# A streaming-encoder trunk: the low parts of the mixing weights formed by an accumulating DMA

## The chip, the cores and the metric

The kernel runs on one core of a Trainium2 chip. The metric is the device time of one execution in microseconds (us): before the change the median of three runs is 1188.21 us (1187.47 to 1188.51). The core has a matrix engine (PE, TensorE), three engines for elementwise work (DVE or VectorE, ACT or ScalarE, POOL or GpSimd), and queues that issue DMA transfers: SP's, and here after the change POOL's as well.

## The reference: what is computed

Two layers on 512 tokens of width 1024, in float32. Each layer has a mixing half and a feed-forward half:

```
h    = rms_norm(x, g_pre_mix)
proj = h @ w_in            # pool 512 | q 512 | k 512 | v 512 | indexer 584
a    = causal pooling mixer (windows 2, 4, 8, 16) @ w_pool * pool_scale
b    = attention of 8 heads over the 128 best keys per query, picked by the indexer
x    = x + rms_norm(concat(a, b) @ w_out, g_post_mix)
h    = rms_norm(x, g_pre_ffn)
x    = x + rms_norm(relu(h @ w_ff1)**2 @ w_ff2, g_post_ffn)
```

## The kernel before

**High and low parts.** PE's operands are F32R tiles, rounded from float32. Each operand is held as two of them: high = the value rounded to F32R, and low = value - high. A product is three matmuls (`mm3`, L825): high x high, high x low, low x high. So each weight has to be loaded, rounded and subtracted before PE may use both parts.

**The weight stream** (`WeightStream`, L420). All weights of both layers pass in a fixed order through one stream: index, q, k, v, pool, output projection (once for each of two pairs of token tiles), then feed-forward. A load brings two chunks of 128 rows (512 KB, or twice 256 KB for the pool weights) into one of NRAW = 2 raw buffers, `wraw`. A chunk is split by `_split` (L519) into one of NWS = 8 weight tiles `ws`, which hold the high part in `[:, 0]` and the low part in `[:, 1]`:

```
self.copy(w[:, 0, :n], raw)                                             # L533
self.tt(w[:, 1, :n], raw, w[:, 0, :n].bitcast(F32), OP.subtract)        # L534
```

`copy` (L656) may go to DVE or to ACT; `tt` (L648) is always DVE. A raw buffer is free again after both subtractions, and `_ahead` then issues the next load on SP's queue. A weight tile is free when its matmuls are done: `ws.done()` splits the next chunk.

**The stages of a layer.** The index projection and the indexer's scores; then q, k and v (`rows_block`, L948: 12 matmuls of 512 columns per chunk), while DVE picks the best keys (`select`, L931, with max and match-replace on tiles `m` and `bias`); `attention(2)`, the pooling mixer, `attention(3)`, `attention(0)`, `attention(1)`; then the output projection `out_pair(1)` and `out_pair(0)` (L1082: 6 matmuls per chunk, since each chunk serves two token tiles), with norms behind each token tile. A norm takes a power on POOL (tile `rstd`, L780). The feed-forward half has other chunks: a part of its weights are sums of blocks (`_combine`, L539, from `uraw`).

**What sets the order.** Every instruction is first recorded with its cost and dependencies (`_Recorder`, L359), then a list scheduler (`Planner`, L83) plans all engines by these costs and latencies in 40 sweeps and issues each engine's instructions in the order of their planned starts (L193). Where there are two ways (`planner.either`, L143), it picks the engine. At run time each engine works through its own list in order and waits where something is not ready.

Profile lines all read L372, the recorder's call; so groups are told apart by tiles: `pg`, `pool`, `pi`, `po`, `s`, `pf`, `one`, `two` are results of matmuls, `pt`, `tr`, `hT` transposes, `early` and `A` left operands.

Of the kernel before, what the change touches and what calls it, by code (L numbers as in the profile page):

```python
# [12 lines left out]
F32 = mybir.dt.float32  # L13
F32R = mybir.dt.float32r
I32 = mybir.dt.int32
AF = mybir.ActivationFunctionType
OP = mybir.AluOpType

P = 128
# [18 lines left out]
POOL_PAIRS = ((2, 3), (0, 1))  # L38
# [44 lines left out]
class Planner:  # L83
# [19 lines left out]
    def __init__(self, nc):  # L103
        self.nc = nc
        self.ops = []
        self.writer, self.readers = {}, {}
        self.rings, self.before, self.first = {}, {}, {}
        self.touched = {}
        self.collected = None
        self.loads = []  # L110
# [75 lines left out]
        self.ops.append((ways, deps, soft - deps))  # L186

    def lag(self, ea, eb):
        if eb == "sp":
            return self.DMA_STARTS  # L190
        return self.DMA_LANDS if ea == "sp" else self.LATENCY.get((ea, eb), 150)

    def issue(self):  # L193
# [13 lines left out]
        for i in range(n - 1, -1, -1):  # L207
            e, cost = ops[i][0][0][:2]
            tail = 0.0
            for j, hard in succ[i]:  # L210
                tail = max(tail, rank[j] + (self.lag(e, ops[j][0][0][0]) if hard else -cost))
            rank[i] = cost + tail
# [146 lines left out]
class _Recorder:  # L359
# [3 lines left out]
    def __getattr__(self, method):  # L363
        def call(*args, **kw):
            out = kw["out"] if "out" in kw else args[0]
            writes = [out] + ([kw["accum_out"]] if kw.get("accum_out") is not None else [])
            if method == "tensor_tensor_reduce":
                writes.append(args[7])
            reads = [a for k, a in list(enumerate(args))[1:] + list(kw.items())
                     if isinstance(a, bass.AP) and k not in ("out", "accum_out") and all(a is not w for w in writes)]  # L370
            way = (self.name, self.cost(method, args, kw, out, reads),
                   lambda: getattr(self.real, method)(*args, **kw), self.port(method, out, reads))  # L372
            if self.planner.collected is not None:
                self.planner.collected.append(way + (writes, reads))
            else:
                self.planner.record([way], writes, reads)
        return call
# [11 lines left out]
    def cost(self, method, args, kw, out, reads):  # L389
        def free(ap):  # L390
            return math.prod(c for _, c in list(ap.ap)[1:])

        def psum(ap):
            return ap.space == bass.MemoryType.PSUM

        n = free(out)
        scalars = sum(free(a) == 1 and n > 1 for a in reads)
        if self.name == "pe":
            if method == "transpose":
                return 59 if args[1].dtype == F32R else 109  # L400
            return max(4.5 + n / 2.25, 111 if free(args[1]) > 64 else 60)
        if self.name == "act":
            accum = kw.get("accum_out") is not None
            return (53 if any(psum(a) for a in reads[:1]) else 93) + n / 1.2 + 93 * (accum + scalars)
        if self.name == "dve":
            if method in ("max", "match_replace"):
                return 70 + 1.04 * free(args[-1] if method == "max" else args[2])
            fast = method in ("tensor_copy", "tensor_scalar") and not any(psum(a) for a in [out] + reads)
            return 70 + (0.52 if fast else 1.04) * n + 60 * scalars
        if self.name == "pool":  # L410
            if method == "memset":
                return 50
            return (70 + 1.2 * n) if method == "tensor_scalar" else (520 if n == 1 else 50 + 2.35 * n)
        nbytes = math.prod(c for _, c in out.ap) * 4
        return max(450.0, nbytes / 360.0)


class WeightStream:
# [5 lines left out]

    COMBINATIONS = ("11", "12", "S2", "S1", "S3", "S4", "22")

    def __init__(self, copy, tt, sp, raw_pool, ws_pool, unit_pool, sum_pool):
        self.copy, self.tt, self.sp = copy, tt, sp
        self.raw_pool, self.ws_pool, self.unit_pool, self.sum_pool = raw_pool, ws_pool, unit_pool, sum_pool
        self.loads = []  # L430
        self.chunks = []
        self.tiles = []
        self.n_load = self.n_split = 0
        self.raw = {}
        self.sums = {}
        self.in_use = {"raw": 0, "unit": 0}
        self.units_allowed = False
# [23 lines left out]
    def add_unit(self, src, r0, c0):  # L461

        k = len(self.loads)
        for cp in range(2):
            self.loads.append((src, r0 + 2 * cp * P, "unit", c0, 512))
        ids = {}
        for name in self.COMBINATIONS:
            ids[name] = []
            for cp in range(2):
                ids[name].append(len(self.chunks))  # L470
                self.chunks.append((k + cp, name, 512))
        return ids

    def preload(self):
        for _ in range(NRAW):
            self._load()
# [42 lines left out]
    def _split(self):  # L519
        i = self.n_split  # L520
        if i >= len(self.chunks):
            return
        k, j, n = self.chunks[i]
        while k >= self.n_load:
            self._load()
        w = self.ws_pool.tile([P, 2, WMAX], F32R, name="ws")
        self.tiles.append(w)
        self.n_split += 1
        if isinstance(j, str):
            self._combine(k, j, w)  # L530
            return
        raw = self.raw[k][:, j, :n]
        self.copy(w[:, 0, :n], raw)  # L533
        self.tt(w[:, 1, :n], raw, w[:, 0, :n].bitcast(F32), OP.subtract)  # L534
        if j == abs(self.loads[k][2]) - 1:
            self.in_use["raw"] -= 1
            self._ahead()
# [48 lines left out]
def hymba_trunk(ctx: ExitStack, tc: tile.TileContext, x, positions, g_pre_mix, w_in, w_pool,  # L586
                pool_scale, w_out, g_post_mix, g_pre_ffn, w_ff1, w_ff2, g_post_ffn, out):
    nc = tc.nc
    planner = Planner(nc)
    pe, act, dve, pool, sp = [planner.engine(n, e) for n, e in (  # L590
        ("pe", nc.tensor), ("act", nc.scalar), ("dve", nc.vector), ("pool", nc.gpsimd), ("sp", nc.sync))]
    ctx.enter_context(tc.manual_schedule())
    ctx.enter_context(nc.allow_non_contiguous_dma("rows of four bytes: positions and scales"))

    def ring(name, bufs, space=bass.MemoryType.SB):
        return _Ring(planner, ctx.enter_context(tc.tile_pool(name=name, bufs=bufs, space=space)), bufs)
# [7 lines left out]
    rawp = ring("rawp", NRAW)  # L604
    wsp = ring("wsp", NWS)
    t8p = ring("t8p", 2)
# [4 lines left out]
    sup = ring("sup", 2)  # L611
# [50 lines left out]
        planner.either(lambda: dve.tensor_scalar(out, a, by, None, op0=OP.mult),  # L662
                       lambda: act.activation(out, a, AF.Copy, scale=by))

    ws = WeightStream(copy, tt, sp, rawp, wsp, t8p, sup)
    plan = []
    for l in range(DEPTH):
        p = {}
        p["idx"] = ws.add(w_in[l], 0, D, OFF_I, IDX_W)
        p["q"] = ws.add(w_in[l], 0, D, OFF_Q, 512)  # L670
        p["k"] = ws.add(w_in[l], 0, D, OFF_K, 512)
        p["v"] = ws.add(w_in[l], 0, D, OFF_V, 512)
        for pair in POOL_PAIRS:
            p["pool", pair] = ws.add_paired(w_in[l], 0, D, OFF_POOL + P * min(pair), 256)
        for pair in (1, 0):
            ids = []
            for kc in OUT_ORDER[::2]:
                a = ws.add(w_out[l], kc * P, 2 * P, 0, 512)
                b = ws.add(w_out[l], kc * P, 2 * P, 512, 512)
                ids += [(kc, a[0], b[0]), (kc + 1, a[1], b[1])]  # L680
            p["out", pair] = ids
        for g in range(4):
            for b in (2 * g, 2 * g + 1):
                p["ff1", b] = ws.add_unit(w_ff1[l], 0, 512 * b) if b else ws.add(w_ff1[l], 0, D, 512 * b, 512)
            for hf in range(2):
                p["ff2", g, hf] = ws.add(w_ff2[l], 1024 * g, 1024, 512 * hf, 512)
        plan.append(p)

    gains = {}
# [180 lines left out]
    for l in range(DEPTH):  # L870
        p = plan[l]
# [15 lines left out]
        for t in range(NT):  # L887
            n = P * (t + 1)
            banks = [psg.tile([P, 512], F32, name="pi", tag="pg")[:, :292] for _ in range(2)]
            for kc in range(KC):  # L890
                w = ws.get(p["idx"][kc])
# [292 lines left out]
        for g in range(4):  # L1184
            f1 = []
            for bi in range(2):
# [7 lines left out]
                ids = p["ff1", blk]  # L1194
# [9 lines left out]
                if blk == 0:  # L1204
                    for tp in (1, 0):
                        cols = slice(256 * tp, 256 * tp + 256)
                        for j in range(4):
                            bank = pq(j, "pf")[:, :256]
                            for kc in range(KC):
                                w = ws.get(ids[kc])  # L1210
# [9 lines left out]
            for hf in range(2):  # L1220
                ids = p["ff2", g, hf]
# [25 lines left out]
        for t in range(NT):  # L1247
# [3 lines left out]
            else:  # L1251
                for hf in range(2):
                    c = slice(512 * hf, 512 * hf + 512)
# [24 lines left out]
```

## Time and profile before

| | |
|---|---|
| median of three runs | 1188.21 us |
| the profiled execution's own time | 1189.19 us |
| its span in the profile | 1187.4 us |
| mean granted PE clock | 0.992 |
| PE busy, share | 1154.9 us, 97% |
| DVE busy, share | 962.8 us, 81% |
| ACT busy, share | 593.5 us, 50% |
| POOL busy, share | 31.5 us, 3% |
| HBM read | 112.27 MB |

Busy PE is not PE at its peak: the ends of matmuls are modelled, so a matmul that starts late can hide inside a busy stretch. That is why the steady time of a matmul is compared with what stretches hold. The granted clock is a share of the full one; a stretch below 1.00 had PE at half speed for a part of it.

### The profile page before, as it was taken

How to read it: one execution, taken by the hardware profiler on the slowest of the kernel's cores; microseconds unless marked ns; L12 is line 12 of the kernel's file. 1: busy time of each engine (PE TensorE's matmuls, PEld its weight loads, DVE VectorE, ACT ScalarE, POOL GpSimd, SP SyncE). 2: the span in 40 equal slices, each digit the busy share in tenths (PEclk: the TensorE clock that was granted, in tenths of full speed). 3: DMA queues.
4: the chain of work that ended last, by engine and by line, in shares of the span. 5: the costliest groups of instructions: out<-in, count | busy, mean ns of one | idle time of the engine just before them, and what ended most of it. 6: DMA issues, size and time to landing. Idle time of an engine off the chain costs nothing.

```text
span 1187.4 us, 18436 instructions
## 1 busy us (share of the span) xinstructions
PE 1154.9 (97%) x6888; PEld 1008.9 (85%) x6888; DVE 962.8 (81%) x2134; ACT 593.5 (50%) x1279; POOL 31.5 (3%) x79
## 2 busy tenths in 40 slices
PE   6999999999999999999999999899999999999997
PEld 6988888789899898899898888777998998988985
DVE  7799999889569579577698999998994785875965
ACT  7545796687226036035275277876760440430621
POOL 2000000010000000000010000001000000000001
PEclk9999998999999999999999999999999999999999
DMA  7221222451423223223233121134542241251231
GB/s 249 71 72 36 71 72 72 142 184 66 161 74 132 95 72 132 82 71 97 60 112 89 54 72 54 54 115 134 160 141 73 71 161 54 72 177 36 72 107 71
DMA packets 62169, 115.55 MB, mean 97 GB/s; under 512 B 5248, under 2 KB 10368, under 8 KB 62080
## 3 DMA queue, kind: packets, MB, share of 16 engines
q1 hardware_dynamic: 62080, 114.38, 30.2%
q8 instruction: 54, 0.88, 0.3%
q14 instruction: 35, 0.29, 0.1%
HBM read 112.27 MB, written 2.10 MB: 96 GB/s over the span
## 4 chain that ended last, share of the span: by engine, by line
PE 61%; DVE 26%; DMA 5%; ACT 4%; issue 3%; POOL 1%; SPq 0%; DVEq 0%; ACTq 0%; POOLq 0%
PE pg L372 33%; PE one L372 9%; PE two L372 7%; DVE ws L372 6%; DVE bias L372 3%; PE pi L372 3%; PE pf L372 3%; DVE m L372 3%; DMA wraw<-in_w_out_dram 2%; DMA uraw<-in_w_ff_dram 2%; DVE mx L372 1%; PE lg L372 1%; DVE s L372 1%; PE po L372 1%; DVE pT L372 1%
## 5 line engine op out<-in xcount | busy, mean ns | idle before, releaser
L372 PE MATMUL pg<-ws,f 128*128 128x512 f32 x768 | 230.5, 394 | 0.0
L372 PE MATMUL pg<-ws,A 128*128 128x512 f32 x864 | 227.5, 401 | 0.9 <-DVE A L372 0.6
L372 ACT ACTIVATE ws<-wraw 128x512 fp32r<-128x512 f32 (+1 forms) x182 | 112.9, 632 | 183.8 <-PE pg L372 127.3
L372 DVE TENSOR_TENSOR ws<-wraw,ws 128x512 fp32r<-128x512 f32 (+1 forms) x288 | 194.4, 689 | 5.9 <-ACT ws L372 3.8
L372 PEld LDWEIGHTS pg<-ws,A 128*128 128x128 f32 x864 | 157.7, 188 | 34.3 <-DVE pn L372 1.6
L372 PE MATMUL pg<-ws,f1h 128*128 128x512 f32 x512 | 167.2, 394 | 0.5 <-ACT fr L372 0.5
L372 PEld LDWEIGHTS pg<-ws,f 128*128 128x128 f32 x768 | 141.1, 188 | 29.0
L372 PEld LDWEIGHTS pg<-ws,f1h 128*128 128x128 f32 x512 | 95.6, 188 | 22.3 <-ACT fr L372 1.0
L372 DVE TENSOR_TENSOR ws<-uraw,ws 128x512 fp32r<-128x512 f32 x168 | 111.7, 686 | 2.0 <-ACT ws L372 0.7
L372 DVE CAST ws<-wraw 128x512 fp32r<-128x512 f32 (+1 forms) x106 | 45.0, 426 | 75.2 <-PE pg L372 64.3
L372 PE MATMUL two<-A,ws 128*128 128x256 f32 x672 | 104.9, 281 | 0.0
L372 PE MATMUL pg<-ws,f1l 128*128 128x512 f32 x256 | 95.8, 393 | 0.0
L372 PEld LDWEIGHTS two<-A,ws 128*128 128x128 f32 x672 | 92.3, 188 | 1.9
L372 ACT ACTIVATE ws<-uraw 128x512 fp32r<-128x512 f32 x95 | 57.7, 627 | 67.8 <-PE pg L372 29.7
L372 ACT ACTIVATE s<-s,st 128x384 f32<-128x384 f32 (+3 forms) x118 | 64.7, 565 | 21.4 <-DVE st L372 20.8
L372 ACT ACTIVATE fr<-fr 128x512 f32<-128x512 f32 (+1 forms) x109 | 63.5, 596 | 21.0 <-DVE fr L372 20.1
L372 DVE TENSOR_TENSOR facc<-pg,facc 128x512 f32<-128x512 f32 x48 | 32.7, 688 | 46.2 <-PE pg L372 46.2
L372 DVE CAST ws<-uraw 128x512 fp32r<-128x512 f32 x73 | 30.4, 424 | 41.7 <-PE pg L372 32.6
L372 PE MATMUL pi<-ws,A 128*128 128x292 f32 x384 | 61.8, 310 | 1.1 <-DVE ws L372 0.8
L372 PE MATMUL pool<-A,ws 128*128 128x512 f32 x192 | 59.2, 405 | 0.0
L372 PEld LDWEIGHTS pg<-ws,f1l 128*128 128x128 f32 x256 | 48.0, 188 | 10.9
L372 PE MATMUL one<-A,ws 128*128 128x256 f32 x336 | 57.0, 280 | 0.0
(189 smaller groups left out, 2203.5 us busy)
## 6 DMA issues: line engine op xcount, KB each, us to landing
wraw<-in_w_ff_dram SPq DMA_DIRECT2D x72, 512.0 KB, 3.8
uraw<-in_w_ff_dram SPq DMA_DIRECT2D x56, 512.0 KB, 4.9
wraw<-in_w_out_dram SPq DMA_DIRECT2D x32, 512.0 KB, 3.7
wraw<-in_w_in_dram SPq DMA_DIRECT2D x24, 512.0 KB, 3.6
wraw<-in_w_in_dram SPq DMA_DIRECT2D x8, 584.0 KB, 4.3
wraw<-in_w_in_dram SPq DMA_DIRECT2D x16, 256.0 KB, 2.9
x<-in_x_dram SPq DMA_DIRECT2D x4, 512.0 KB, 6.5
out_dram<-x SPq DMA_DIRECT2D x8, 256.0 KB, 2.1
```

Source lines behind the costliest of these rows:

```text
L372: lambda: getattr(self.real, method)(*args, **kw), self.port(method, out, reads))
```

## The change

For the weights of q, k, v, the pooling mixer and the output projection (64 chunks a layer, 128 in all; the index weights and the feed-forward weights stay as they were), the subtraction on DVE is replaced. ACT writes the negated high part into the low half of the tile, and a DMA issued from POOL's queue reads the same rows of the weight from HBM once more and adds them to it: low = -high + weight. The raw buffer is now read by the copy alone. The planner gets a sixth queue, `gq`, for POOL's DMAs, with a cost of 1200 per transfer and a lag of 2500 behind it (in the planner's nanoseconds); it keeps `gq` and `pool` apart, though both are one queue on the chip.

```
     def lag(self, ea, eb):
+        if ea == "gq":
+            return 2500
+        if eb == "gq":
+            return 200
         if eb == "sp":
             return self.DMA_STARTS
...
+            reads = ([out] if kw.get("accum_op") is not None else []) + [a for k, a in ...
...
+        if self.name == "gq":
+            return 1200
...
+    def low_by_dma(self, ids):
+        self.by_dma.update(self.chunks[i][0] for i in ids)
...
         self.copy(w[:, 0, :n], raw)
-        self.tt(w[:, 1, :n], raw, w[:, 0, :n].bitcast(F32), OP.subtract)
+        src, r0, count, c0, ncols = self.loads[k]
+        if k in self.by_dma:
+            high, low = w[:, 0, :n], w[:, 1, :n]
+            self.act.activation(low, high.bitcast(F32), AF.Copy, scale=-1.0)
+            rows = src[r0 + j * P:r0 + (j + 1) * P, c0:c0 + ncols]
+            if count < 0:
+                low = low.rearrange("p (c n) -> p c n", c=2)
+                rows = src[r0 + 2 * j * P:r0 + 2 * (j + 1) * P, c0:c0 + ncols].rearrange("(c p) n -> p c n", p=P)
+            self.gq.dma_start(low, rows, accum_op=OP.add)
+        else:
+            self.tt(w[:, 1, :n], raw, w[:, 0, :n].bitcast(F32), OP.subtract)
...
+    gq = planner.engine("gq", nc.gpsimd)
...
+        for name in ("q", "k", "v"):
+            ws.low_by_dma(p[name])
+        for pair in POOL_PAIRS:
+            ws.low_by_dma(p["pool", pair])
+        for pair in (0, 1):
+            ws.low_by_dma([i for _, *halves in p["out", pair] for i in halves])
```

How the planner's order changes. First DVE in layer 0, where the best keys are picked and the first attention runs. `ws<-wraw,ws` is a subtraction, `ws<-wraw` a rounding copy, `m` and `bias` the selection, `s` the scores of attention. Before:

```order
L372 MATCH_REPLACE bias<-m_317,bias 128x512
L372 TENSOR_SCALAR bias<-bias 128x384
L372 MAX m_317<-bias 128x8
L372 ISA s,st<-s,bias 128x384
L372 ISA st 128x1
L372 TENSOR_TENSOR ws<-wraw,ws 128x512
L372 MATCH_REPLACE bias<-m_317,bias 128x512
L372 ISA s,st<-s,bias 128x384
L372 ISA st 128x1
L372 TENSOR_TENSOR ws<-wraw,ws 128x512 x2
```

And with the change, at the corresponding place:

```order
L376 ISA s,st<-s,bias 128x384
L376 ISA st 128x1
L376 MAX m_317<-bias 128x8
L376 CAST ws<-wraw 128x512
L376 MATCH_REPLACE bias<-m_317,bias 128x512
L376 RECIPROCAL st<-st 128x1
L376 MATCH_REPLACE bias<-m_372,bias 128x256
```

The subtractions between the steps of the selection are gone; in their place stands now and then a copy that ACT did before. Over the whole program 128 subtractions go, and DVE's copies of 128x512 from `wraw` to `ws` are 140 where they were 101, its scalings of `s` (TENSOR_SCALAR) 38 where they were 10; ACT's fall by the same numbers.

Second, POOL's queue from the indexer's last fill of layer 0 (`sc`) to the second layer's first. Before there was nothing but fills and the powers of the norms:

```order
L372 MEMSET sc 64x64 x4
L372 MEMSET mx 128x16 x3
L372 TENSOR_TENSOR rstd<-rstd,neg_half 128x1 x8
L372 MEMSET mx 128x16
L372 TENSOR_TENSOR rstd<-rstd,neg_half 128x1 x8
```

With the change, from the last fill but two of `mx` in layer 0 (`ws<-in_w_out_dram` is an accumulating transfer):

```order
L376 DMA ws<-in_w_out_dram 128x512 x4
L376 MEMSET mx 128x16
L376 DMA ws<-in_w_out_dram 128x512 x2
L376 MEMSET mx 128x16
L376 DMA ws<-in_w_out_dram 128x512 x15
L376 TENSOR_TENSOR rstd<-rstd,neg_half 128x1
L376 DMA ws<-in_w_out_dram 128x512 x3
L376 TENSOR_TENSOR rstd<-rstd,neg_half 128x1 x2
L376 DMA ws<-in_w_out_dram 128x512 x8
L376 TENSOR_TENSOR rstd<-rstd,neg_half 128x1 x5
```

The powers of the first norms now stand between and behind the transfers of the output weights, each of which waits for its negation on ACT.

## Rows read from the trace of the kernel before

**Rows 1.** Page, part 1: busy us, share of the span, instructions.

```profile
span 1187.4 us, 18436 instructions
PE 1154.9 (97%) x6888; PEld 1008.9 (85%) x6888; DVE 962.8 (81%) x2134; ACT 593.5 (50%) x1279; POOL 31.5 (3%) x79
```

**Rows 2.** Windows: start:end, length; busy us (instructions) per engine; granted clock; DMA share; GB/s.

```profile
60.00:195.00 135.00, 132.85 (x685) 109.72 (x684) 130.69 (x374) 91.88 (x203) 0.86 (x5) 0.96 0.21 63
195.00:255.00 60.00, 58.96 (x322) 47.94 (x320) 54.81 (x147) 44.04 (x119) 5.91 (x6) 1.00 0.41 127
640.00:775.00 135.00, 131.43 (x687) 108.34 (x686) 131.16 (x369) 84.47 (x182) 0.64 (x5) 0.99 0.20 60
775.00:835.00 60.00, 58.14 (x298) 45.34 (x297) 55.80 (x162) 41.92 (x117) 4.52 (x5) 1.00 0.44 133
270.00:580.00 310.00, 307.77 (x1929) 276.14 (x1928) 225.88 (x391) 112.99 (x201) 0.11 (x1) 1.00 0.29 95
```

**Rows 3.** Chain of waits, longest pieces: start us, us, engine, tile, count.

```profile
...
288.18 2.85 PE one L372 x24
...
297.17 37.12 PE pg L372 x160
...
```

**Rows 4.** Groups, PE, 60 to 255: busy us, mean ns, then idle before.

```profile
L372 PE MATMUL pg<-ws,A 128*128 128x512 f32 x400 | 105.3, 403 | 0.1
L372 PE MATMUL pool<-A,ws 128*128 128x512 f32 x96 | 30.5, 405 | 0.0
L372 PE MATMUL po<-pT,vS 128*128 128x256 f32 x120 | 23.5, 308 | 0.6 <-DVE pT L372 0.4
L372 PE MATMUL s<-kS,qT 128*128 128x384 f32 (+3 forms) x64 | 17.9, 343 | 0.3 <-ACT qT L372 0.2
L372 PE MATMUL pg<-ws,early 128*128 128x512 f32 x48 | 15.4, 408 | 0.0
L372 PE MATMUL pt<-ident,s 128*128 128x128 f32 x80 | 15.0, 279 | 0.1
```

**Rows 5.** Chain of waits by line, 60 to 200, then 640 to 780.

```profile
by line: DVE bias L372 15.4%; DVE m L372 12.8%; PE pg L372 11.3%; DVE ws L372 9.1%; DVE mx L372 6.1%; DVE s L372 5.3%; issue 5.3%; DVE pT L372 4.0%; DVE sc L372 4.0%; PE po L372 3.9%; ACT s L372 3.6%; DVE rt L372 2.2%; DVE early L372 1.9%; 
...
by line: PE pg L372 13.6%; DVE bias L372 13.5%; DVE m L372 10.2%; DVE ws L372 7.2%; DVE mx L372 6.3%; issue 5.9%; DVE s L372 5.8%; DVE pT L372 4.4%; DVE early L372 2.7%; PE tr L372 2.6%; DMA wraw<-in_w_in_dram 2.6%; DMA wraw<-in_w_out_dram 
```

**Rows 6.** Windows at the end of layer 0's attention to the last blocks.

```profile
165.00:180.00 15.00, 13.63 (x83) 11.43 (x82) 14.90 (x46) 14.77 (x33) 0.23 (x2) 0.94 0.11 36
180.00:195.00 15.00, 14.69 (x68) 12.47 (x68) 13.96 (x52) 8.88 (x32) 0.00 (x0) 0.72 0.22 70
```

**Rows 7.** Groups over the whole span, weight tiles: busy us, mean ns, idle before.

```profile
L372 DVE TENSOR_TENSOR ws<-wraw,ws 128x512 fp32r<-128x512 f32 (+1 forms) x288 | 194.4, 689 | 5.9 <-ACT ws L372 3.8
L372 ACT ACTIVATE ws<-wraw 128x512 fp32r<-128x512 f32 (+1 forms) x182 | 112.9, 632 | 183.8 <-PE pg L372 127.3 <-DMA wraw<-in_w_ff_dram 28.3 <-DMA wraw<-in_w_out_dram 13.3
L372 DVE CAST ws<-wraw 128x512 fp32r<-128x512 f32 (+1 forms) x106 | 45.0, 426 | 75.2 <-PE pg L372 64.3 <-DMA wraw<-in_w_ff_dram 5.3 <-DMA wraw<-in_w_out_dram 2.9
```

**Rows 8.** Page, part 6: DMA issues, count, KB each, us to landing.

```profile
wraw<-in_w_out_dram SPq DMA_DIRECT2D x32, 512.0 KB, 3.7
...
wraw<-in_w_in_dram SPq DMA_DIRECT2D x16, 256.0 KB, 2.9
```

**Rows 9.** Tile ws, PE, 223 to 250: count, ns, first and last start.

```profile
L372 PE MATMUL pg<-ws,A x96: 387/394/497, 224.0 to 248.2; 128*128 128x512 f32 x96
```

**Rows 10.** Windows of the output projection and the stretch behind it.

```profile
195.00:225.00 30.00, 29.41 (x167) 23.46 (x166) 27.75 (x95) 24.54 (x74) 0.67 (x1) 1.00 0.35 107
224.00:250.00 26.00, 25.57 (x123) 20.59 (x123) 23.06 (x45) 16.13 (x37) 2.81 (x5) 1.00 0.53 163
255.00:270.00 15.00, 13.02 (x106) 12.28 (x105) 12.75 (x21) 11.13 (x26) 1.50 (x3) 1.00 0.79 269
```

**Rows 11.** Groups over the whole span: the powers on POOL.

```profile
L372 POOL TENSOR_TENSOR rstd<-rstd,neg_half 128x1 f32<-128x1 f32 x32 | 27.8, 874 | 570.1 <-DVE rstd L372 564.8 <-ACT f1h L372 5.3
```

More of the change, by code (lines that the diff above doesn't have):

```diff
@@ L368, in call @@
                 writes.append(args[7])
-            reads = [a for k, a in list(enumerate(args))[1:] + list(kw.items())
+            reads = ([out] if kw.get("accum_op") is not None else []) + [a for k, a in list(enumerate(args))[1:] + list(kw.items())
                      if isinstance(a, bass.AP) and k not in ("out", "accum_out") and all(a is not w for w in writes)]
@@ L425, with __init__ @@
     COMBINATIONS = ("11", "12", "S2", "S1", "S3", "S4", "22")
-    def __init__(self, copy, tt, sp, raw_pool, ws_pool, unit_pool, sum_pool):
-        self.copy, self.tt, self.sp = copy, tt, sp
+    def __init__(self, copy, tt, act, sp, gq, raw_pool, ws_pool, unit_pool, sum_pool):
+        self.copy, self.tt, self.act, self.sp, self.gq = copy, tt, act, sp, gq
+        self.by_dma = set()
         self.raw_pool, self.ws_pool, self.unit_pool, self.sum_pool = raw_pool, ws_pool, unit_pool, sum_pool
@@ L663, in scaled @@
                        lambda: act.activation(out, a, AF.Copy, scale=by))
-    ws = WeightStream(copy, tt, sp, rawp, wsp, t8p, sup)
+    ws = WeightStream(copy, tt, act, sp, gq, rawp, wsp, t8p, sup)
     plan = []
```

## The prediction

> **What bounds the kernel now.** I read the busy table first [rows 1]: PE 1154.9 of 1187.4 us, DVE 962.8, ACT 593.5, POOL 31.5. That says PE, but it is an average over unlike stages, so the stage windows come next [rows 2]. In the feed-forward stretch 270 to 580 PE is busy 307.8 of 310 us and DVE 225.9: PE alone bounds it, and the change leaves its weights as they were. In the mixing stages DVE is as full as PE: 130.7 of 135 us in 60 to 195 and 131.2 in 640 to 775, where ACT has 92 and 84 us.
>
> How much PE time is lost there? In a stretch where nothing is missing, 160 matmuls of 512 columns take 37.12 us, 0.232 each, and 24 of 256 columns 2.85 us, 0.119 each [rows 3]. From 60 to 255 layer 0 has 1006 matmuls (685 + 322 in the windows, one counted twice) [rows 2]. The large groups [rows 4] are 400 + 96 + 48 = 544 of 512 columns (126.2 us), 120 of 256 (14.3), 64 score products of mean width 320 (0.145 each, 9.3) and 80 transposes. I price these 80 and the 198 others, mostly transposes, at 0.119 (33.1): an estimate. Sum 182.9 of 195 us, so about 12 us of PE time are lost in layer 0's mixing stage. Layer 1's stretch has fewer matmuls in the same length, so about as much: 24 us in all, the ceiling for any gain here.
>
> Who causes it: the chain of waits restricted to each stretch [rows 5]. From 60 to 200 it is mostly DVE: top-k selection (bias 15.4%, m 12.8%), then the weights' own tiles, ws 9.1% of 140 us = 12.7 us; in layer 1 7.2% = 10.1 us. Where that chain ends, the clock shows it: in 165 to 180 PE is busy only 13.63 of 15 us, and in the next 15 us the granted clock is 0.72 [rows 6], that is 8.4 us at the lower of the two levels (1.2 instead of 2.4 GHz), 4.2 us of work lost. It is part of the 12.
>
> **The change part by part.**
>
> Removed: 64 subtractions a layer on DVE (24 for q, k, v, 8 for pool, 32 for the output projection). One takes 0.689 us [rows 7]: 44.1 us a layer, 88.2 us in all.
>
> Added on ACT: 64 negations a layer of 128x512, an ACTIVATE as the copy of 0.632 us in the same group of rows: 40.4 us a layer. ACT is idle 195 - 91.9 - 44.0 = 59 us of layer 0's stretch [rows 2], so it fits, but tightly. The order shows how the planner pays: over the program it moves 39 weight copies from ACT to DVE (101 to 140 casts, 0.426 each [rows 7], +16.6 us) and some 28 scalings of the softmax rows (at most a cast each by the same row, +12 us). DVE keeps a net relief of 88.2 - 16.6 - 12 = 60 us, 30 a layer.
>
> Of that 30 only what lies on the chain counts. The ws share, 12.7 and 10.1 us, is copies and subtractions; the subtractions' part goes, the moved copies come back, and after some 12 us PE is the bound whatever DVE does. Bounds: 0 (what is late next is ACT, now with the negations ahead of its exponentials) to 12 us a layer. I take 8, nearer to the chain's rows: **-16 us**.
>
> Moved: each chunk's low part now passes copy, ACT, POOL's queue and a transfer of 256 KB before PE may use it. The trace has no such transfer. The nearest row is a plain load of 256 KB, 2.9 us from issue to landing; 512 KB take 3.7 [rows 8]. An accumulating one also reads its target, so I bound it by 2.9 and, twice that, 5.8 us. One chunk of q, k, v or pool feeds 12 matmuls, 2.8 us of PE, and eight weight tiles are held, so a chunk can be started some 19 us ahead; for these stages even 5.8 + 0.6 us hides, if the transfers overlap. If that cover were gone, it would be the wait of rival B.
>
> The output projection is where it is tight. A chunk feeds only 6 matmuls, 1.39 us. In layer 0's second half of it 96 matmuls take from 224.0 to 248.2 [rows 9], 24.2 us against 22.3 at the steady rate: nearly no slack. In that stretch the 16 DMA engines are already busy 0.53 of the time at 163 GB/s [rows 10], which makes 308 GB/s at a full share; the row of 255 to 270 (0.79 at 269 GB/s) makes 340. Sixteen more chunks are 4.2 MB, as much as the stretch moves now (163 GB/s x 26 us = 4.2 MB). If an accumulating byte costs what a loaded one does, the share becomes 1.06: full, +1.6 us. If it costs twice, 1.59: +15 us. Below nothing: a raw buffer is free after the copies, two subtractions (1.4 us) earlier, so loads start sooner; at most the 1.9 us that PE loses here come back. The first half (195 to 225, share 0.35 [rows 10]) has room for 16 chunks at the lower price, 0.35 + 0.45; at the higher, 1.25, some would be late, beside attention's own matmuls. So -2 to +15 us a layer; I take 4, nearer to the copy's price since the eight held tiles let half of the chunks go ahead: **+8 us**.
>
> What else the transfers are queued with: on POOL the rstd powers of the norms now stand behind accumulating transfers, each of which waits for its negation. In layer 0 one power stands behind 15 transfers to the output weights, two behind three more, and five behind the last eight. A power takes 0.874 us [rows 11] and the norm after it feeds the first feed-forward matmuls. The last transfer must be issued about 4 us before its matmul anyway, so the powers behind it are due in time; cost taken as 0, up to 3 us a layer if a transfer holds POOL longer. SP's loads keep their order and queue; they share the 16 engines, which is the term above.
>
> Sum: profiled execution 1189.2 us (span 1187.4 plus 1.8 around it) - 16 + 8 = 1181.2. The profiled run lies 1.0 above the median of the three runs, 1188.2, so I predict **1180 us**.
>
> **Rivals.**
>
> A, the forecast: DVE relief of 5 to 12 us a layer, output projection dearer by 0 to 6: between 1188.2 - 24 = 1164 and 1188.2 - 10 + 12 = 1190; by itself 1170 to 1187. Chance 0.42.
>
> B, slower: the accumulating transfers set the pace of the output projection. It decides once POOL and the DMA engines need more than about 1.9 us per chunk (32 chunks in the 60 us of 195 to 255). At 2.9 us one after another, without overlap, 32 take 93 us: +33 a layer, far above the gain; at 2.3 us 74 us, +14 a layer, 1188.2 - 16 + 28 = 1200. For it: nothing in the trace shows that POOL can issue at such a rate (its 31.5 us of work are tiny instructions [rows 1]). Against: SP's loads of 512 KB overlap today. Time 1192 to 1225, likeliest 1200. Chance 0.24.
>
> E, slower by less: POOL cannot prepare a transfer while DVE runs a cast. DVE's casts take 0.426 us each [rows 7] and there are 140 of them in the changed order; if each of the 16 transfers of a tight stretch loses one, that is 6.8 us a layer there, 1188.2 - 16 + 8 + 13.6 = 1194. The Trainium skill, page "SBUF — State Buffer", section "SBUF: two separate sides", states this rule: a DMA issued from the GpSimd queue needs descriptors that GpSimd writes itself, and an fp32 copy on VectorE from SBUF to SBUF locks it out until the copy has ended, plus about 115 ns. By that page's figure the price would be 8.7 us a layer, an estimate. No run shows it yet, since this kernel issues no transfer from POOL. Chance 0.08.
>
> C, nothing: the planner gives DVE other work in place of the subtractions and ACT becomes late in the same chain, or the two terms cancel: 1188 within 2.4 us. For it: ACT would be at (136 + 40 - 21) / 195 = 0.79 on average (the moved work of both layers, 39 x 0.632 + 28 x 0.6 = 41 us, halved), and its waits for DVE in attention are dependencies, not load. Chance 0.14.
>
> D, more: the whole 24 us of lost PE time come back, with no half clock, and the transfers cost nothing: 1164, or down to 1160 with the 1.9 us a layer of the projection. Against: dependencies inside attention stay. Chance 0.12.
>
> **How the numbers follow.** A change of 0.2% (2.4 us) is about what a measurement of this kernel can tell from none. Faster by more: A nearly whole (0.40) and D (0.12): 0.52. Within: C's 0.14 and a sliver of A: 0.15. Slower: B, E and the rest of A: 0.33. The range should leave out 0.2: above 1210 the serial end of B, about 0.12, below 1163 half of D and a little more. So 1163 to 1210; A's own range is 1170 to 1187.
>
> **What would show it.** Right: DVE busy falls by about 60 us and ACT rises by about 40; in 60 to 195 the chain's DVE ws share is gone and the granted clock stays at 1.00; the output projection's 96 matmuls take 25 to 31 us. B shows as PE or its weight loads waiting on transfers into ws, a landing time above 6 us, and a DMA share near 1 there. The forecast is wrong if DVE falls and PE's lost time does not (C), or if POOL's queue holds the norms and the first feed-forward matmuls start later after the last output matmul than now.

## The result and the profile after

The changed kernel took 1222.44 us, median of four runs (1216.17 to 1225.98), beside 1188.36 us for the kernel before on the same chip: ratio 1.028, 95% interval 1.024 to 1.033. It is slower by 34 us; the prediction was 1180, range 1163 to 1210. The profiled execution took 1216.17 us.

The page after, parts 1, 3 and 6. Part 3 gives packets, MB and the time of the packets as a share of 16 DMA engines' span; q1 is SP's queue, q0 is POOL's, the new one. Part 6 is as in [rows 8].

```profile
span 1214.4 us, 18705 instructions
PE 1157.9 (95%) x6888; PEld 1008.4 (83%) x6888; DVE 926.8 (76%) x2101; ACT 615.8 (51%) x1312; POOL 146.6 (12%) x207
...
q1 hardware_dynamic: 62080, 114.38, 28.9%
q0 software_dynamic: 20480, 33.56, 17.3%
...
ws<-in_w_in_dram POOLq DMA_DIRECT2D x64, 256.0 KB, 5.3
wraw<-in_w_out_dram SPq DMA_DIRECT2D x32, 512.0 KB, 5.4
ws<-in_w_out_dram POOLq DMA_DIRECT2D x64, 256.0 KB, 6.2
wraw<-in_w_in_dram SPq DMA_DIRECT2D x24, 512.0 KB, 5.0
wraw<-in_w_in_dram SPq DMA_DIRECT2D x8, 584.0 KB, 4.2
wraw<-in_w_in_dram SPq DMA_DIRECT2D x16, 256.0 KB, 4.5
```

Against [rows 1], DVE lost 36 us of work, ACT gained 22 and POOL 115 (the forecast had about -60 on DVE and +40 on ACT). The new number is in part 3. q1 moves 114.38 MB in 28.9% of 1214.4 us, 3.07 us of all 16 engines per MB; q0 moves 33.56 MB in 17.3%, 6.26 us per MB: **an added byte costs 2.04 times a loaded one**. The transfers land after 5.3 and 6.2 us, and the raw loads beside them are late too: the output weights' 512 KB take 5.4 us in place of 3.7 [rows 8].

Windows of after: the first q chunks, the mixing stage, then the two halves of the output projection in layer 0 and the second half in layer 1 (columns as in [rows 2]):

```profile
40.00:60.00 20.00, 16.63 (x107) 14.36 (x106) 11.11 (x32) 11.03 (x25) 7.60 (x10) 1.00 0.90 206
60.00:195.00 135.00, 131.32 (x708) 109.14 (x707) 128.03 (x389) 102.17 (x226) 32.08 (x37) 1.00 0.62 124
190.00:226.00 36.00, 33.23 (x182) 26.73 (x181) 25.67 (x97) 28.79 (x81) 12.04 (x14) 1.00 0.82 179
226.00:261.00 35.00, 29.84 (x117) 22.80 (x117) 19.97 (x44) 17.78 (x40) 13.79 (x17) 0.85 0.92 214
...
822.00:860.00 38.00, 28.65 (x122) 20.93 (x120) 20.17 (x42) 20.66 (x47) 13.52 (x17) 0.96 0.89 205
```

The half clock of [rows 6] is gone from 60 to 195 (1.00 in place of 0.96 [rows 2]). But behind it the DMA share is 0.92 where [rows 10] had 0.53, PE is busy 29.84 of 35 us, and the granted clock falls to 0.85 there: a part of the stretch ran at the lower level, 1.2 GHz. The tile rows that answer to [rows 9], of 225.7 to 261.2:

```profile
L376 PE MATMUL pg<-ws,A x96: 387/397/793, 225.7 to 261.0; 128*128 128x512 f32 x96
its engine sat idle before it (us, times) until:
  DMA ws<-in_w_out_dram: 5.2, 4
```

The same 96 matmuls take 35.3 us where they took 24.2; in layer 1 37.4 where they took 26.2. These two stretches hold 22.3 of the 27.0 us by which the span grew. The chain of waits back from 855 us, in layer 1, shows what they wait for (start us, us, what):

```profile
824.51 0.43 DVE ws L376
824.94 0.02 SPq L376
824.96 0.03 issue
825.00 8.38 DMA wraw<-in_w_out_dram
...
834.59 0.35 DVE ws L376
834.93 0.02 issue
834.95 7.18 DMA wraw<-in_w_out_dram
...
842.26 0.44 DVE ws L376
...
843.25 0.62 ACT ws L376
...
844.37 0.87 POOL ws L376
...
847.34 1.85 issue
849.19 6.26 DMA ws<-in_w_out_dram
```

Two raw loads of 8.38 and 7.18 us stand one after the other, each issued only after the copy that freed its buffer; then copy, negation, POOL's issue and a transfer of 6.26 us. The raw loads, which the change didn't touch, are the longest pieces. The waits of the whole span, engine and tile, then us, times and longest:

```profile
POOL ws L376 <- issue: 22.1, 12, 4.8
...
DVE ws L376 <- DMA wraw<-in_w_out_dram: 20.5, 9, 4.9
PEld pg L376 <- DMA ws<-in_w_out_dram: 18.1, 10, 3.1
PE pg L376 <- DMA ws<-in_w_out_dram: 14.1, 8, 2.7
...
PEld pool L376 <- DMA ws<-in_w_in_dram: 7.9, 5, 3.2
...
PEld pg L376 <- DMA ws<-in_w_in_dram: 3.3, 3, 1.9
```

The first line is time in which POOL stood idle before an issue with nothing in the profile that ended its wait. 11 of these 12 waits ended 0.25 to 0.31 us after the third-last transfer had landed, and no issue found more than two earlier transfers still in flight. So in this trace POOL's queue has at most three of these transfers under way, and the next issue waits for a landing.

### The profile page after: what moved, and what is told of

The parts are those of the page before. It is cut to its first block, busy times and chain, and to the rows that moved or that the text cites. A ratio compares the mean times of both kernels' runs of the same rounds, so it can differ in the third digit from the quotient of the medians.

```text
span 1214.4 us, 18705 instructions
## 1 busy us (share of the span) xinstructions
PE 1157.9 (95%) x6888; PEld 1008.4 (83%) x6888; DVE 926.8 (76%) x2101; ACT 615.8 (51%) x1312; POOL 146.6 (12%) x207
## 3 DMA queue, kind: packets, MB, share of 16 engines
q1 hardware_dynamic: 62080, 114.38, 28.9%
q0 software_dynamic: 20480, 33.56, 17.3%
## 5 line engine op out<-in xcount | busy, mean ns | idle before, releaser
L376 PE MATMUL pg<-ws,A 128*128 128x512 f32 x864 | 236.6, 410 | 19.0 <-DMA ws<-in_w_out_dram 14.1
L376 ACT ACTIVATE ws<-wraw 128x512 fp32r<-128x512 f32 (+1 forms) x142 | 88.8, 633 | 159.7 <-DVE facc L376 65.1
L376 PEld LDWEIGHTS pg<-ws,f 128*128 128x128 f32 x768 | 141.2, 188 | 28.9
L376 DVE CAST ws<-wraw 128x512 fp32r<-128x512 f32 (+1 forms) x146 | 61.8, 428 | 112.7 <-PE pg L376 74.8
L376 DVE TENSOR_TENSOR ws<-wraw,ws 128x512 fp32r<-128x512 f32 (+1 forms) x160 | 108.6, 694 | 5.1 <-ACT ws L376 2.9
L376 ACT ACTIVATE ws<-ws 128x512 fp32r<-128x512 f32 x128 | 78.0, 628 | 31.5 <-DVE ws L376 30.5
L376 POOL DMA_DIRECT2D ws<-in_w_in_dram x64 | 62.7, 985 | 184.6 <-ACT ws L376 97.6
L376 ACT ACTIVATE ws<-uraw 128x512 fp32r<-128x512 f32 x87 | 53.2, 627 | 57.7 <-PE pg L376 25.8
L376 POOL TENSOR_TENSOR rstd<-rstd,neg_half 128x1 f32<-128x1 f32 x32 | 24.1, 769 | 448.1 <-DVE rstd L376 448.1
L376 POOL DMA_DIRECT2D ws<-in_w_out_dram x64 | 57.7, 938 | 103.1 <-ACT ws L376 36.7
L376 PE MATMUL pool<-A,ws 128*128 128x512 f32 x192 | 62.8, 421 | 7.5 <-DMA ws<-in_w_in_dram 7.4
```

## Experiments

Sixteen kernels. "The changed order" is that of the changed kernel, instruction by instruction; the others were planned anew. Ratios are to the kernel before on the same chip, with 95% intervals; 1% is 11.9 us.

**No transfer**, changed order. The transfer is not issued, and ACT writes zero (scale 0.0), so the low parts are missing.

```
-  lambda: getattr(self.real, method)(*args, **kw), ...
+  lambda: None if self.name == "gq" else getattr(self.real, method)(*args, **kw), ...
```

> The changed kernel's order on PE, DVE, ACT and SP, without the 128 accumulating transfers (their issue on POOL is left out, and the negation's scale is 0 instead of -1, so that the low parts of these weights are zero). If the transfers are the whole loss (theory T: the DMA engines, or theory L: the longer way of each chunk), this lies below the kernel before, at 1165 to 1182, by what DVE's relief is worth. If the planner's new order, with the negations on ACT, is itself at fault (theory O), it stays at 1188 or above, up to 1222.

1173.65 us, 0.989 (0.987 to 0.991). So DVE's relief is real, 12.7 us, and without transfers the changed order is not at fault. Its windows of the output projection in layer 0, to be held against those above:

```profile
183.00:216.00 33.00, 32.63 (x184) 27.04 (x183) 26.54 (x99) 29.44 (x84) 0.00 (x0) 1.00 0.30 96
216.00:242.00 26.00, 24.78 (x118) 19.85 (x117) 18.91 (x42) 17.12 (x40) 3.78 (x5) 1.00 0.51 161
```

From none to all transfers the ratio moves by 0.039, 47 us. The next kernels divide these.

**Plain transfer**, changed order. `accum_op` is dropped, so a transfer overwrites the low half with the weights.

> The changed kernel's order on all engines, but the 128 transfers overwrite the low part with the weights instead of adding them (so the low parts are wrong). T, an accumulating byte takes the DMA engines about twice a loaded one's time and fills them in the output projection: 1190 to 1207, and the share of the queue of POOL's transfers falls from 17.3% to 8 or 9%. L, the length of each chunk's way (copy, negation, POOL, landing) is what PE waits for, whatever the transfer does: 1215 to 1224.

1185.47 us, 0.999 (0.997 to 1.000). Its POOL queue, the second half of its output projection in layer 0, and POOL's unexplained waits:

```profile
q0 software_dynamic: 20480, 33.56, 10.5%
```

```profile
217.00:246.00 29.00, 25.70 (x118) 19.61 (x117) 18.96 (x43) 17.32 (x40) 9.71 (x16) 1.00 0.84 254
```

```profile
POOL ws L376 <- issue: 1.0, 4, 0.3
```

The same bytes, packets and issues cost 12 us, not 47: 10.5% of 1181.0 us is 3.70 us per MB. Adding accounts for the other 35. The time fell below the expected range, and the queue's share above the expected 8 or 9%. Up to four earlier plain transfers were in flight at an issue, so holding POOL back at three goes with the adding too.

**Only q, k, v and pool** (the lines below go), and **only the output projection** (the other four lines of `low_by_dma` go), planned anew:

```
-        for pair in (0, 1):
-            ws.low_by_dma([i for _, *halves in p["out", pair] for i in halves])
```

> Only q, k, v and the pooling mixer's weights by transfer, the output projection's subtracted on DVE as before, planned anew. From the stages of the changed kernel's profile the second half of the output projection holds 22 of the 27 us lost: then 1185 to 1195 (T and L alike). If the earlier stages lose as much as they gain through waits on their first transfers, 1188; if the forecast's gain of 8 us a layer is there, 1175 to 1182.

> Only the output projection's weights by transfer, the others subtracted on DVE as before, planned anew. T and L: the loss of the output projection alone, 1205 to 1222. O (order everywhere) would spread the loss: about 1205 here and as much in the kernel without it.

1191.47 us, 1.004 (1.003 to 1.006), and 1215.89 us, 1.024 (1.022 to 1.026). Against the kernel before, most of the loss belongs to the output projection; how the 47 us against no transfers divide is read in the changed order below.

**Half the chunks**, planned anew (`if k in self.by_dma and i % 2 == 0`): in the output projection alone, then everywhere.

> Transfers only in the output projection, and there only for every second chunk (64 in place of 128); the other chunks' low parts are subtracted on DVE as before. Before on this chip 1186.4 us; the output projection alone with all its transfers 1215.9. Theory T (time of the DMA engines: in the changed kernel an accumulated MB took 17.3% of 1214.4 us / 33.56 MB = 6.26 us of all 16 engines, a loaded one 28.9% of 1214.4 / 114.38 = 3.07 us; a layer's output projection moves 8.39 MB of each, 78 us, against about 62 us of matmuls; with half the transfers 52 us, which fits): the stall goes nearly whole, not by half; second half of the output projection 24 to 27 us a layer, 1182 to 1192 us. Theory L (each transfer is late by its landing of 6 us, whatever the engines' load): half the stalls stay, half of +29.5: 1198 to 1206 us, second half about 30 us.

> The change for every second chunk of q, k, v, pool and the output projection (64 transfers of 128). Theory T: no stage is full any more (6.2 us of DMA engines per MB of weights, where the steady matmuls of the same MB leave 7.4); DVE's relief is worth about half of the 12.7 us that it gave without transfers, less some waits at the first q chunks: 1178 to 1188 us. Theory L: half of the +36 us that the whole change costs stays: 1198 to 1210 us.

1194.49 us, 1.004 (1.002 to 1.006): of 1.024 a sixth is left, not half, which is just above theory T's range; but the second halves took 29.5 and 28.2 us, near theory L's 30 and not T's 24 to 27. And 1201.37 us, 1.011 (1.009 to 1.014), at the low end of theory L. Neither theory fits both, and each kernel has a new plan, so the changed order was used from here on.

**The planner given the measured price**: `return 2500` becomes 5700, `return 1200` becomes 1640.

> The change as it is, with the planner's two numbers for a transfer set to what the trace showed: 1640 in place of 1200 for its time on the queue (0.262 MB at 6.26 us per MB), and 5700 in place of 2500 for its landing. Theory O (the order planned with too small numbers is at fault): at least half of the +36 us comes back, below 1204 us. Theory T (the bytes and their price are the same): 1212 to 1230 us, and the second half of the output projection stays above 33 us a layer.

1209.25 us, 1.017 (1.015 to 1.019): between the two ranges. Some 13 us come back with this plan; 20 remain.

**Adding from SBUF**: each transfer reads the raw buffer (`rows = raw`) and not HBM.

> The change as it is, but each transfer adds from the raw buffer in SBUF in place of reading the weights from HBM a second time; so a raw buffer is held until the transfer has read it. Theory H (the second read of HBM is what costs: with plain transfers the same bytes cost half as much because nothing waits on HBM twice): the share of the transfers' queue falls towards that of plain ones (10.5%), and the time below 1205 us. Theory T (the adding itself, in the DMA engines at the SBUF side, costs): the share stays at 15 to 19%, and the time at 1212 us or above, up to 1250, since raw buffers come free later by a landing of about 5 us and two of them is all there is.

1244.04 us, 1.047 (1.044 to 1.051). q0 takes 16.1% of 1241.5 us, 5.96 us per MB: reading HBM a second time isn't the price. With the plain transfers' 3.70 that points to the adding; a plain transfer out of SBUF was not run.

**How many, how large, where**: four kernels in the changed order, with ACT writing zero. One leaves out every second transfer, one sends 64 of 128 rows in each (`args = [a[:64] for a in args]`), one leaves out those of q, k, v and pool; later one sent 8 rows in each. Low parts are incomplete in all.

> The changed kernel's own order, instruction by instruction, with every second of the 128 transfers not issued (the low parts are then not the real ones: ACT writes zero, and only every second tile has something added). In this order no transfer gave ratio 0.989 to before and all 128 gave 1.028, 46 us between them. Theory L (each transfer brings its own delay): half of the 46 us, about 1198 us at before = 1188 (1192 to 1204). Theory T (the DMA engines are the bound in the stages with transfers; with half of the adding bytes the output projection needs 52 us of them a layer against 60 of matmuls): at most a quarter of the 46 us, 1174 to 1186.

> The changed kernel's own order with all 128 transfers, each of 64 rows in place of 128 (half the bytes and half the descriptors; the low parts are then not the real ones). Theory T (bytes): as with every second transfer left out, 1174 to 1186 us. Theory N (a fixed price for each transfer, its issue on POOL and its landing): nearer to the whole change than to no transfers, 1198 to 1220.

> The changed kernel's own order, with the transfers of q, k, v and pool not issued and those of the output projection as they are (low parts not the real ones). The stretch of the output projection's second half lost 9 to 11 us a layer; if the whole of the loss arises within the output projection itself, this gives 1173.7 + 2 x 11 to 14, 1196 to 1202 us; if the early stages' transfers carry their delay into it, or have most of the 46 us themselves, below 1192.

> The changed kernel's own order with all 128 transfers, each of 8 rows in place of 128, a sixteenth of the bytes (the low parts are then not the real ones). Theory N (a price for each transfer whatever its size: its issue on POOL of about 0.9 us and its landing): between 64 rows (1.0059) and somewhat below, 1186 to 1196 us. Theory T (bytes): near no transfers at all (0.989), 1172 to 1180 us.

| transfers | ratio | us above none (difference x 1188) |
|---|---|---|
| none | 0.989 (0.987 to 0.991) | 0 |
| 128 of 8 rows | 0.990 (0.989 to 0.991) | 1 |
| 64 whole, every second | 1.002 (1.001 to 1.003) | 15 |
| 128 of 64 rows | 1.006 (1.004 to 1.008) | 20 |
| 64 whole, all in the output projection | 1.010 (1.008 to 1.013) | 25 |
| 128 whole | 1.028 (1.024 to 1.033) | 47 |

The number of transfers alone costs nothing that can be measured; the bytes added do (packets fell with them here, but the plain transfers had all bytes and packets for 12 us), and more than in proportion: the first half 15 to 20 us, the second 27 to 32. Where they stand matters: the same 64 cost 15 spread out and 25 in one stage. Every second transfer and 64 rows both came out between their two theories, so fitting into the engines' time isn't quite free: with every second, in the second half of the output projection the share was still 0.80 and 0.74, and the 96 matmuls took 29.1 us in both layers.

The transfers of the output projection alone landed in the range expected "if the whole of the loss arises" there, but that reading doesn't hold: 25 of 47 us are there, and adding the transfers of q, k, v and pool brings the other 21. With every second transfer and with 64 or 8 rows POOL's unexplained waits were 0, 1.4 and 1.0 us, so the first 15 to 20 us come without any holding back.

**Nobody waits for the landing**, changed order, all transfers. PE reads the high part where it should read the low one (`swap` leads from the one to the other):

```
+        if self.name == "pe":
...
+            args = [swap[id(a)][1] if id(a) in swap else a for a in args]
```

> The changed kernel's own order with all 128 transfers issued as they are, but PE reads the high part where it should read the low part of these tiles, so that no matmul waits for a transfer's landing (the product is then not the real one). Theory W (what costs is that matmuls wait for landings of 5 to 6 us): nearly all of the 46 us goes, 1172 to 1182 us. Theory C (the transfers' load on the DMA engines delays the raw loads that the copies wait for, 20.5 us of DVE's waits): most of it stays, 1200 to 1222.

1203.34 us, 1.014 (1.012 to 1.015), at the foot of theory C. Removing the matmuls' waits gives back 17 us; 29 of the 47 remain. The second halves of its output projection, the tile rows of the first, and the chain there:

```profile
222.70:257.90 35.20, 27.22 (x118) 21.58 (x119) 21.64 (x46) 18.86 (x44) 13.89 (x17) 0.91 0.96 226
811.90:846.40 34.50, 27.49 (x120) 21.25 (x119) 20.79 (x44) 20.61 (x46) 13.23 (x17) 0.90 0.95 226
```

```profile
L387 PE MATMUL pg<-ws,A x96: 387/396/775, 222.7 to 257.5; 128*128 128x512 f32 x96
```

```profile
by line: DMA wraw<-in_w_out_dram 29.5%; DMA wraw<-in_w_ff_dram 12.1%; issue 10.3%; PE pf L387 8.3%; DVE ws L387 6.8%; ACT ws L387 5.0%; POOL rstd L387 4.2%; PE hT L387 4.2%; PE pg L387 3.6%; ACT h L387 3.1%; DVE pn L387 2.8%; ACT pn L387 2.
```

PE depends on no transfer here, and no wait of any engine ends on one. Yet the 96 matmuls took 34.8 and 34.2 us, nearly as long as in the changed kernel (35.3 and 37.4; without transfers 26.3 and 26.0). The DMA engines are busy 0.96 and 0.95 of the time, and raw loads lead the chain: in layer 0 three of them took 8.08, 5.79 and 5.68 us, where [rows 8] has 3.7 for the output weights. PE's own long waits there, 6.2 and 6.1 us, are for transposes behind a norm, and in layer 0 the norm's steps on DVE stood behind copies that waited 4.9 and 3.3 us for raw loads. So the larger part of the loss comes through the raw loads, which share the engines. Not all of it need: POOL was held 25.1 us here too, and in layer 0 the chain has one such wait, 1.6 us before an issue with two powers of a norm behind it.

**A new plan by itself**: the kernel before with seed 54 in place of 53.

> The kernel before with the planner's seed 54 in place of 53: how much a new plan of the same work moves the time by itself. If it stays within 0.3% of before (1185 to 1192 us), the kernels that were planned anew (every second chunk, the output projection alone) can be read to 4 us; if it moves by more, by that much less.

1189.80 us, 1.002 (1.001 to 1.003). One other plan moved the time by 0.2%; it doesn't bound what plans of changed work may do.

**The subtraction on POOL**, no transfers and no negation, for all chunks or every second (`gq` is then POOL's own queue of instructions).

```
+            self.gq.tensor_tensor(w[:, 1, :n], raw, w[:, 0, :n].bitcast(F32), op=OP.subtract)
```

> No transfers and no negation: the low parts of the same 128 chunks are subtracted on POOL, planned anew. The planner reckons 1253 ns for one such subtraction, a figure that no run has shown yet. If DVE's relief (worth 12.7 us in the changed order without transfers) is kept, since a subtraction moves no bytes over the DMA engines: 1172 to 1182 us. If POOL is too slow for the output projection, which needs a chunk every 0.75 us there (64 chunks in about 48 us), or its reads slow DVE's: above 1190, up to 1230.

> The same for every second chunk only; the others are subtracted on DVE. POOL then needs one subtraction per 1.5 us in the output projection. If about half of DVE's relief is kept: 1178 to 1184 us. If POOL and DVE slow each other: within 0.4% of before or above, 1184 to 1200.

1213.98 us, 1.023 (1.021 to 1.024), and 1203.56 us, 1.013 (1.011 to 1.014), the second above both of its ranges. POOL's group in the first, and DVE's subtractions in the second:

```profile
L376 POOL TENSOR_TENSOR ws<-wraw,ws 128x512 fp32r<-128x512 f32 x128 | 176.3, 1389 | 204.0 <-ACT ws L376 119.1 <-DVE ws L376 55.3 <-issue 12.1
...
L376 DVE TENSOR_TENSOR ws<-wraw,ws 128x512 fp32r<-128x512 f32 (+1 forms) x224 | 159.4, 725 | 8.0 <-ACT ws L376 5.8
```

1.389 us for one, twice DVE's 0.689 [rows 7]. In the first kernel none of DVE's own 160 subtractions ran beside one on POOL, so their 0.696 us says nothing about how the two engines affect each other; in the second, 19 did and took 1.09 us on average, the other 128x512 ones 0.69. DVE was not relieved either: in the first the new plan gave it other work, 969.3 us in all. What share of the loss each has was not separated. Of these sixteen, no kernel that computes the whole reference was faster than the one before.

## Why the prediction was wrong

**The step that failed is the output projection's term, "+4 a layer".** The two shares were worked out, 1.06 if an accumulating byte costs what a loaded one does and 1.59 if it costs twice, with +1.6 and +15 us. I took 4, "nearer to the copy's price since the eight held tiles let half of the chunks go ahead". Part 3 of the page shows 2.04 times, and the second half cost 11.1 and 11.2 us a layer against before, 9.0 and 11.4 against the kernel without transfers (26.3 and 26.0 us); with the first half, 3.3 and 2.8, the whole projection cost 12.3 and 14.2. The upper bound, +15, was the near one. Eight tiles did not let half of the chunks go ahead: no more than three transfers were in flight. And going ahead can't help when the whole stage is full: 8.39 MB of loads and 8.39 MB of added bytes need 8.39 x (3.07 + 6.26) = 78 us of the DMA engines a layer, and without transfers the stage lasts 59 (183.0 to 242.2). I had bounded a transfer by its landing and asked whether that hides; what decides is the engines' time summed over a stage, which has no such cover.

**Hidden transfers of q, k, v and pool: failed as much, taken as 0.** From the start of the mixing half to the last pool matmul, the changed kernel lost 6.6 us in layer 0 and 8.9 in layer 1 against the one without transfers; leaving out these transfers saved 21 us (1.028 to 1.010). A lead of 19 us covers one landing of 5.3 us, but not the first q chunks, where nothing is ahead yet and the share is 0.90 (40 to 60), nor the pool weights, where PE's weight loads waited 7.9 us. By the runs in the changed order the three terms are -12.7 (DVE), +25 (output projection) and +21 (q, k, v and pool, added last), where the sum had -16, +8 and 0.

**DVE's relief, -16 us: right within its bounds.** Without transfers the time was 12.7 us lower, and from the start of a layer to the middle of its output projection, 8.1 and 6.4 us less passed than before. By its parts it was rougher: DVE's work fell by 36 us, not 60. The subtractions left as counted (194.4 to 108.6), the moved copies came as counted (45.0 to 61.8), but some 33 us of other work, not 12, came on top, 10.2 of it the softmax scalings (10 to 38).

**The powers behind the transfers, 0: right.** The 32 powers took 24.1 us, and from the last output matmul to the end of the first feed-forward group passed 28.7 and 29.2 us (before: 30.8 and 28.4). In the kernel in which nobody waits for a landing, a power behind a held transfer did come onto the chain, by 1.6 us.

**Rivals.** B came true, with its three signs (landing above 6 us, share near 1, PE waiting on transfers into ws), and at 1222 within its 1192 to 1225. Its threshold of 1.9 us a chunk was passed in two ways. The engines' time is 0.262 MB x 9.33 = 2.45 us a chunk. And POOL's issue takes 0.94 us, but with three in flight and the next issue 0.31 us after a landing, 6.2 us to landing make (6.2 + 0.31) / 3 = 2.2 us a chunk, an estimate. What it lacked is that the waiting comes mostly through the raw loads. E is not the cause: in the kernel with 8 rows in each transfer the 128 issues hold POOL almost as long as in the changed one (0.85 and 0.92 us on average, there 0.99 and 0.94) beside the same casts, and the whole of it costs 1 us. Issue by issue the traces say the same: in the changed kernel 33 issues that overlapped a cast of DVE's by more than 0.1 us took 0.94 us on average, the other 95 took 0.97; with 8 rows 37 took 0.94, the other 91 0.86. So a cast added less than 0.1 us to an issue. If there is a lock as the Trainium skill has it ("SBUF — State Buffer", "SBUF: two separate sides"), no run here shows it holding an issue for the length of a cast. C and D didn't occur.

Another page has a price that the runs here come out above. The Trainium skill, "DMA: Bandwidth & Descriptors", section "Anatomy of one DMA — SWDGE (gpsimd) path", fits a transfer from this queue as 2.0 us plus its bytes at 436 GB/s, an estimate of 2.6 us for 256 KB. The accumulating ones landed after 5.3 and 6.2 us beside other loads, the plain ones of the same order after 3.7 and 4.8; the measurement decides.

**What stays open.** The 17 us of waits and the 29 of slowed loads interact, so they aren't two independent prices. Why POOL is held at three accumulating transfers, and how much of the loss that is rather than the busy engines, wasn't shown. The lower clock can have cost at most 0.15 x 35 = 5.3 us in 226 to 261 and 0.04 x 38 = 1.5 us in 822 to 860, an estimate; layer 1 lost as much with the smaller part, so the clock isn't the main cause, but what made it fall wasn't separated. Nor was it shown why the plan with the measured price recovers 13 us.

## What to carry to other kernels

Before moving arithmetic from an engine into transfers, add up the DMA engines' time over each stage, every queue together, and hold the sum against the stage's length; a landing time that hides says nothing when the engines are full. If an operation's price is known only within a factor of two and the stage fills at the upper end, the sum should stand at the upper end. And the first victims are the transfers that were already there: look for loads that got slower, not only for waits on the new ones.

## What the runs showed of the hardware

- An accumulating transfer of float32 from HBM into a float32r tile took 6.26 us of the 16 DMA engines per MB, a plain one on the same queue with the same packets 3.70, a load on SP's queue 3.07. In the other kernels with whole accumulating transfers from HBM it was 5.9 to 6.8. With its source in SBUF the accumulating one still took 5.96.
- Landing hung on the bytes in all more than on the size of one: in the output projection 256 KB landed after 6.2 us with all transfers and after 5.3 with every second, 128 KB after 5.1 with all, 16 KB after 3.8.
- At most three whole accumulating transfers were in flight in any kernel, and up to five plain, 64-row or 8-row ones. Where POOL was held, the next issue mostly came 0.3 us after a landing; these waits were 22.1 us in the changed kernel and 1.0 with plain transfers.
- 19 subtractions on DVE that ran beside one on POOL took 1.09 us on average, the others of the same kernel 0.69.
- An accumulating issue held POOL 0.94 to 0.99 us on average, with a sixteenth of the rows 0.85 to 0.92; a plain one of the same size 0.54 to 0.60.
